# Trunk layer in fp32 on one core: where the row sums of the shared MLP pieces stand in the engines' order, and 64 weight columns in two HGRN2 products

## The chip, the cores and the metric

The kernel runs on one core of a Trainium2 chip. The metric is the device time of one execution in microseconds (us). The time before is the median of three runs. A profiled execution has its own time; its trace gives, for every engine, when each instruction began, how long it took and what ended the idle time before it. The engines are PE (TensorE matmuls, with PEld for its weight loads), DVE (VectorE), ACT (ScalarE), POOL (GpSimd) and SP (SyncE, which here only issues DMAs). ACT issues DMAs too.

## What is computed

One layer of a hybrid encoder over 1024 tokens of width 1024, with 16 meta tokens in front. One input projection feeds three mixers: HGRN2 (6 heads of 64), Mamba-2 (6 heads) and S5 (16 groups). Their outputs are concatenated, projected by w_out, added to the scaled input and normalised; a squared-ReLU MLP of width 4096 and a second normalisation follow.

```python
proj = h @ w_in[l]
q_a, f_a, i_a, g_a, z_b, xbc_b, dt_b, u_c = jnp.split(proj, split_idx, axis=-1)
...
mixed = jnp.concatenate([y_a, y_b, y_c], axis=-1).astype(h.dtype) @ w_out[l]
h = layer_norm(ALPHA * h + mixed, ln1_g[l], ln1_b[l])
ff = jnp.square(jax.nn.relu(h @ w_mlp_in[l])) @ w_mlp_out[l]
h = layer_norm(ALPHA * h + ff, ln2_g[l], ln2_b[l])
```

HGRN2 works in chunks; inside a chunk, token t reads token s with a decay that depends on both and on the key dimension:

```python
o_inter = jnp.einsum('bhtk,bhkv->bhtv', qc * jnp.exp(G), state)
diff = G[:, :, :, None, :] - G[:, :, None, :, :]
decay = jnp.exp(jnp.where(causal[:, :, None], diff, -jnp.inf))
scores = jnp.einsum('bhtsk,bhsk->bhts', qc[:, :, :, None, :] * decay, kc)
o_intra = jnp.einsum('bhts,bhsv->bhtv', scores, vc)
```

## The kernel before

**Products in three matmuls.** fp32 numbers are split into a high and a low half of a shorter type. `mm3` (L107 to L110) multiplies with three matmuls: high weight by high data (L108), high by low (L109), low by high (L110). A row of the trace names them as output<-moving operand, weights. Here `hi`, `lo`, `h1b`, `fh` and `fl` are such halves; `pm_o`, `pg`, `pm_sc` are PSUM tiles. `pm_o` and `pm_sc` have two buffers each and `pg` three.

**Weights.** `load_raw` (L182) has SP load a block of 128 by 512 (256 KB) into `raw`, a ring of four buffers. `split` has ACT cast the high half (L100), then DVE subtract to get the low half (L87). A raw buffer comes free when its low half is made.

**Order.** All engines work in order. The tile scheduler sets the order of instructions on each engine when the kernel is built; a row that waits holds everything behind it on its engine, and a DMA issue on SP that waits for a buffer holds the issues behind it.

**Stages.** Tokens are in two halves of 512. Until some 340 us the input projection, S5 and the first half of HGRN2 and Mamba-2 run together; until some 440 us w_out of half 0 and its layer norm; until some 650 us the second half of HGRN2 and Mamba-2 beside four MLP pieces of half 0 (512 hidden units each). Eight HGRN2 chunks of 128 tokens are handled in all. Then w_out of half 1 follows: `wout_units(1, ...)` gives eight sums, the four token tiles t4 to t7 for the first 512 columns (dh0), then the same for dh1; each is 24 matmuls and ends in an accumulate on DVE, `acc<-acc,pm_o` (L90). The layer norms and transposes (`norm1`, `h1_transpose`) of half 1 run beside the last eight sums of the pieces of half 0. Then piece 0 of half 1: its products with w_mi, and eight sums with w_mo of 12 matmuls each.

**Shared pieces.** From about 778 us pieces 4 to 7 are computed for both halves at once by a Strassen scheme (`up_strassen`). It needs differences and sums of blocks of the two halves' activations, the row sums, made by `row_sums` (L1246): `fetch3` loads two blocks of `b_d` (the stored activations) into `ar`, a pool of eight buffers; `third` subtracts one from the other on DVE, splits the result on ACT and DVE, and ACT stores both halves to `T_d` number 3. `first`, `second` and `fourth` make the others. `stream(n)` (L1239) has SP read `T_d` number n back into the `h1a` tiles, four loads of 512 KB. Weight differences are made beside: `w5` adds two raw w_mi blocks on DVE into `tw` (L84), which is then split.

**Where the row sums stand before.** `run(a, b)` interleaves two lists of units in the order of the code: the eight w_out sums and the eight units of `fetch3` and `third`. In piece 0 a string of letters sets the order by hand: u and w are its products, f and n the units of `first` and `second`, s is `stream(1)`, and d its eight sums.

**HGRN2's levels.** `hg_level` computes the scores of a chunk by levels of width 1 to 64. Levels below 64 use 64 weight columns on each half of the array, `ps[hms[x]]` (L791). The last level (L783) uses 64 weight columns and 128 moving ones, on one half only, and ACT copies the result to `Py` (L785). `hg_out` (L810) sums q times k per token by two moving columns, `ind2`, with 128 weight columns.

Of the kernel before, what the change touches and what calls it, by code (L numbers as in the profile page):

```python
# [66 lines left out]
def tile_trunk(ctx, tc, xT, x_tok, w_vdt, w_ch, w_out, w_mi, w_mo, glu_w, pack, kconst,  # L67
# [15 lines left out]
    def add(e, out, a, b):  # L83
        e.tensor_tensor(out=out, in0=a, in1=b, op=ALU.add)  # L84

# [3 lines left out]
    def stt(out, a, s, b, op0, op1):  # L89
        V.scalar_tensor_tensor(out=out, in0=a, scalar=s, in1=b, op0=op0, op1=op1)  # L90

# [90 lines left out]
    def load_raw(src):  # L182
        rings.append(rings.pop(0))
        raw = rings[-1]()
        nc.sync.dma_start(out=raw, in_=src)
        return raw

    def load_h(src, dst=None):
# [588 lines left out]
    def hg_level(c, h):  # L777
        hb = HB[c % len(HB)]
        ps = p_sc()
        if h == 64:  # L780

            for ct in range(3):
                PE.matmul(ps[0:64, ct * 128:ct * 128 + 128].rearrange("p (g l) -> p g l", g=2),  # L783
                          hb["B"][:, ct, 0:64], hb["A"][:, ct, :, 64:128], start=True, stop=True, skip_group_check=True)
            S.copy(hb["Py"][0:64], ps[0:64, 0:384].rearrange("p (h l) -> p h l", h=6))  # L785
        else:
# [18 lines left out]
    def hg_out(c):  # L805
# [3 lines left out]
        for ct in range(3):  # L809
            PE.matmul(po[:, 384 + 2 * ct:386 + 2 * ct], hb["QK"][:, ct], ind2, start=(ct == 0), stop=False,  # L810
                      skip_group_check=True)
        for h in range(6):
# [261 lines left out]
    def mix_in(half, k):  # L1074
        src_d, o = ((mixA_d, 0), (mixB_d, 3), (mixC_d, 6))[k // 3]
        raw = load_raw(src_d[:, k - o, HALF * half:HALF * half + HALF])
        split(hk(half, 0, POS[k]), hk(half, 1, POS[k]), raw)

    def accumulate(t, dh, lhs, w, first, c0=0, nc_=512):

        cs = slice(512 * dh + c0, 512 * dh + c0 + nc_)
        ps = p_o()[:, 0:nc_]
        n = len(w)
        for j in range(n):
            mm3(ps, lhs[j][0], lhs[j][1], w[j][0][:, c0:c0 + nc_], w[j][1][:, c0:c0 + nc_], j == 0, j == n - 1)
        if first:
            stt(acc[t][:, cs], acc[t][:, cs], ALPHA, ps, ALU.mult, ALU.add)
        else:
            add(V, acc[t][:, cs], acc[t][:, cs], ps)

# [155 lines left out]
    def row_sums(t2h, t2l, pool):  # L1246
# [38 lines left out]
        def units(f):  # L1285
            return [lambda k=k: f(k) for k in range(4)]

        return units(fetch3) + units(third), units(first) + [lambda: stream(1)] + units(second), units(fourth)

    def up_strassen(js, A, t2, again, ahead, beside):  # L1290

# [77 lines left out]
        def keep(f, half):  # L1369
            return lambda i, p: S.copy(tile_(f, half, i), p)  # L1370
# [7 lines left out]

        us += [w5] + go("c", "s1", "1", True, keep(1, 0)) + [lambda: stream(3)] + beside[:2]
        us += [w1] + go("a", "11", "11", True, keep(0, 1)) + beside[2:]  # L1380
# [8 lines left out]

    def strassen_units(fs, ts_, keep, b_op, sums=None, again=False, beside=()):  # L1390

# [162 lines left out]
        if sums is not None:  # L1554
            us += up_strassen(js, A, sums, again, ahead, list(beside))
        else:
# [110 lines left out]
    sums = row_sums(t2h, t2l, ff2)  # L1667
    run(wout_units(1, (6, 7, 0, 1, 2, 3, 4, 5), True), sums[0])
    run(sum([[lambda t=t: norm1(t), lambda t=t: h1_transpose(t)] for t in h1_], []), pre[cut:])
# [3 lines left out]
    p0 = piece(0, [1], (), HALF, True)  # L1673
    for c in "u u f u w f u f f d d s n d n d n d n d d d".split():
        (p0 if c in "udw" else sums[1]).pop(0)()
    for p in range(NPRE, NP):
        js = list(range(NF * p, NF * p + NF))
        for f in strassen_units((js[:2], js[2:]), (list(h0), list(h1_)), True, lambda name: [None] * 2, (t2h, t2l), p < NP - 1,
                                sums[2] if p == NPRE else ()):
            f()  # L1680
# [110 lines left out]
```

## Time and profile before

| | |
|---|---|
| three runs | 1223.6, 1224.56 and 1226.91 us |
| median | 1224.56 us |
| profiled execution, its own time | 1227.8 us |
| its span, first to last instruction | 1225.7 us |
| mean granted TensorE clock | 0.994 |
| HBM traffic | 148.43 MB read, 30.24 MB written |

A row of a timeline gives the start, the duration, engine and line, the operation, output<-input, the size and, in brackets, how long the engine was idle before it and what ended that. A matmul row lasts longer than the step to the next one, since matmuls overlap: the pace is read from starts. An fp32 matmul that is not split in halves stands as two instructions in the trace. An SP row's duration is the time from its first issue to its last.

### The profile page before, as it was taken

To read this page: it belongs to the slowest core of one execution; us is meant where nothing else is said; L and a number is where in the kernel's file an instruction comes from. 1 tells how busy PE (TensorE), PEld (TensorE's weight loads), DVE (VectorE), ACT (ScalarE), POOL (GpSimd) and SP (SyncE) were. 2 spreads that over 40 slices of the span, in tenths; PEclk is the share of its full clock that TensorE was granted. 3 is DMA by queue.
4 is the path that set the end of the run, shared out by engine and by line. 5 is a ranking of instruction groups with operands and counts; after the bars stand their busy time and mean duration, and the time that the engine had idled before them with its cause. 6 is when DMAs were issued, how large, how long until landed. Compare 5 with 4: busy or idle time off the path is not lost.

```text
span 1225.7 us, 19167 instructions
## 1 busy us (share of the span) xinstructions
PE 1194.5 (97%) x6932; PEld 984.8 (80%) x6932; DVE 898.6 (73%) x1953; ACT 596.0 (49%) x1312; POOL 24.5 (2%) x35
## 2 busy tenths in 40 slices
PE   8999999999999999999998998999999999999997
PEld 8988788778787888887886886878878778788886
DVE  7824866787777797757564776779597796899956
ACT  5343233544775376545453354463553635546542
POOL 0000000000000000000000000000000000003003
PEclk9999999999999999999998999999999999999999
DMA  8142343224557252323159367863635627357331
GB/s 272 55 148 86 78 122 114 104 85 131 164 187 233 65 151 81 100 79 113 52 170 324 100 180 235 266 198 103 237 106 188 224 71 252 124 160 243 121 112 68
DMA packets 111693, 180.97 MB, mean 148 GB/s; under 512 B 10992, under 2 KB 45424, under 8 KB 111600
## 3 DMA queue, kind: packets, MB, share of 16 engines
q1 hardware_dynamic: 108144, 173.47, 44.5%
q10 hardware_dynamic: 3456, 6.29, 1.3%
q8 instruction: 54, 0.88, 0.3%
q14 instruction: 39, 0.32, 0.1%
HBM read 148.43 MB, written 30.24 MB: 146 GB/s over the span
## 4 chain that ended last, share of the span: by engine, by line
PE 70%; DMA 13%; DVE 11%; ACT 3%; issue 2%; SPq 1%; ACTq 0%; POOL 0%; POOLq 0%; DVEq 0%
PE pg L108 11%; PE pg L109 11%; PE pg L110 11%; PE pm_o L108 7%; PE pm_o L109 7%; PE pm_o L110 7%; DMA raw<-w_mi 4%; PE pm_sc L109 2%; PE pm_sc L110 2%; PE pm_sc L108 2%; PE pm_sc L791 2%; DMA raw<-w_out 2%; DVE lo L87 1%; DMA xr<-xT 1%; DMA raw<-w_mo 1%
## 5 line engine op out<-in xcount | busy, mean ns | idle before, releaser
L87 DVE TENSOR_TENSOR lo<-raw,hi 128x512 fp32r<-128x512 f32 x260 | 177.1, 692 | 120.4 <-ACT hi L100 117.3
L100 ACT CAST hi<-raw 128x512 fp32r<-128x512 f32 x260 | 159.1, 619 | 181.7 <-PE pg L109 79.5
L108 PE MATMUL pm_o<-hi,fh 128*128 128x512 f32 x232 | 94.0, 405 | 3.6 <-DVE acc L90 3.3
L110 PE MATMUL pm_o<-hi,fl 128*128 128x512 f32 x232 | 91.6, 395 | 0.0
L109 PE MATMUL pm_o<-lo,fh 128*128 128x512 f32 x232 | 91.6, 395 | 0.0
L108 PE MATMUL pg<-x0h,hi 128*128 128x264 f32 (+1 forms) x264 | 85.3, 323 | 0.4 <-ACT uch L640 0.4
L108 PE MATMUL pg<-h1a,hi 128*128 128x512 f32 (+1 forms) x224 | 82.7, 370 | 2.2 <-ACT hi L100 1.4
L110 PE MATMUL pg<-x0h,lo 128*128 128x264 f32 (+1 forms) x264 | 84.5, 320 | 0.1
L109 PE MATMUL pg<-x0l,hi 128*128 128x264 f32 (+1 forms) x264 | 83.9, 318 | 0.0
L109 PE MATMUL pg<-h1a,hi 128*128 128x512 f32 (+1 forms) x224 | 81.2, 363 | 0.7 <-DMA h1a<-T_d 0.7
L110 PE MATMUL pg<-h1a,lo 128*128 128x512 f32 (+1 forms) x224 | 81.4, 364 | 0.0
L110 PE MATMUL pg<-h1b,lo 128*128 128x512 f32 x176 | 68.6, 390 | 0.1
L108 PE MATMUL pg<-h1b,hi 128*128 128x512 f32 x176 | 68.5, 389 | 0.0
L109 PE MATMUL pg<-h1b,hi 128*128 128x512 f32 x176 | 68.5, 389 | 0.0
L109 PE MATMUL pg<-x1l,hi 128*128 128x512 f32 x168 | 66.4, 395 | 0.0
L110 PE MATMUL pg<-x1h,lo 128*128 128x512 f32 x168 | 66.3, 395 | 0.0
L108 PE MATMUL pg<-x1h,hi 128*128 128x512 f32 x168 | 66.2, 394 | 0.0
L84 DVE TENSOR_TENSOR acc<-acc,pm_o 128x512 f32<-128x512 f32 (+1 forms) x77 | 52.0, 675 | 18.6 <-PE pm_o L110 17.6
L100 ACT CAST fh<-ar 128x512 fp32r<-128x512 f32 (+1 forms) x72 | 39.5, 560 | 40.5 <-DVE ar L87 32.0
L100 ACT CAST hi<-tw 128x512 fp32r<-128x512 f32 x52 | 31.9, 620 | 51.4 <-DVE tw L87 28.9
L108 PEld LDWEIGHTS pm_o<-hi,fh 128*128 128x128 f32 x232 | 44.1, 190 | 13.4 <-DVE acc L90 3.8
L108 PEld LDWEIGHTS pg<-x0h,hi 128*128 128x128 f32 x264 | 49.6, 188 | 5.2 <-ACT uch L640 0.8
(459 smaller groups left out, 3042.7 us busy)
## 6 DMA issues: line engine op xcount, KB each, us to landing
raw<-w_mo SPq DMA_DIRECT2D x140, 256.0 KB, 3.4
raw<-w_mi SPq DMA_DIRECT2D x112, 256.0 KB, 3.3
h1a<-T_d SPq DMA_DIRECT2D x48, 512.0 KB, 6.4
raw<-w_ch SPq DMA_DIRECT2D x48, 256.0 KB, 3.3
raw<-w_out SPq DMA_DIRECT2D x32, 256.0 KB, 3.8
acc<-x_tok SPq DMA_DIRECT2D x8, 512.0 KB, 5.5
b_d<-sig SPq DMA_DIRECT2D x16, 256.0 KB, 3.0
ar<-b_d SPq DMA_DIRECT2D x16, 256.0 KB, 5.3
```

What stands on the lines that cost most here:

```text
L84: e.tensor_tensor(out=out, in0=a, in1=b, op=ALU.add)
L87: e.tensor_tensor(out=out, in0=a, in1=b, op=ALU.subtract)
L100: S.copy(hi, src)
L108: PE.matmul(out, wh, xh, start=start, stop=False, **kw)
L109: PE.matmul(out, wh, xl, start=False, stop=False, **kw)
L110: PE.matmul(out, wl, xh, start=False, stop=stop, **kw)
L791: PE.matmul(ps[hms[x], ct * 64:ct * 64 + 64].rearrange("p (g b l) -> p g b l", g=2, l=h), hb["B"][:, ct, hms[x]], Av, start=True, stop=Tru ...
```

## The change

Four things are done. `load_raw` now keeps its last DMA in `fetched`, and `accumulate` keeps each accumulate's instruction in `sums_done`; `behind(f, n)` issues the units of `f` after the accumulate n places before the latest. `tc.issue_after` adds order on the same engine alone, no wait.

1. Five of the eight w_out sums are written first. The four `fetch3` units stand behind the last w_out load on SP. Each `third` stands behind the accumulate two before the latest that is written (`sums_done[-3]`).
2. `stream(1)` leaves piece 0's string and stands in the first shared piece behind `w5`; there, `w5` stands behind the fifth of the eight accumulates of piece 0 (`sums_done[-4]` when it is written).
3. HGRN2's last level uses, per pair of heads, two matmuls of 64 weight and 64 moving columns, one on each half of the array, and two copies to `Py` in place of one.
4. The q times k sums use 64 weight columns on each half, 6 matmuls in place of 3.

```diff
-        nc.sync.dma_start(out=raw, in_=src)
+        fetched[0] = nc.sync.dma_start(out=raw, in_=src)
         return raw
...
             for ct in range(3):
-                PE.matmul(ps[0:64, ct * 128:ct * 128 + 128].rearrange("p (g l) -> p g l", g=2),
-                          hb["B"][:, ct, 0:64], hb["A"][:, ct, :, 64:128], start=True, stop=True, skip_group_check=True)
-            S.copy(hb["Py"][0:64], ps[0:64, 0:384].rearrange("p (h l) -> p h l", h=6))
+                for g in range(2):
+                    PE.matmul(ps[hms[g], ct * 64:ct * 64 + 64], hb["B"][:, ct, 0:64], hb["A"][:, ct, g, 64:128],
+                              start=True, stop=True, skip_group_check=True)
+            Pg = hb["Py"].rearrange("p (c g) l -> p c g l", g=2)
+            for g in range(2):
+                S.copy(Pg[0:64, :, g], ps[hms[g], 0:192].rearrange("p (c l) -> p c l", c=3))
...
-            PE.matmul(po[:, 384 + 2 * ct:386 + 2 * ct], hb["QK"][:, ct], ind2, start=(ct == 0), stop=False,
-                      skip_group_check=True)
+            for x in hms:
+                PE.matmul(po[x, 384 + 2 * ct:386 + 2 * ct], hb["QK"][:, ct, x], ind2, start=(ct == 0), stop=False,
+                          skip_group_check=True)
...
+    sums_done = []
+
+    def behind(f, n):
+
+        with tc.issue_after(sums_done[-1 - n].ins):
+            f()
...
         if first:
-            stt(acc[t][:, cs], acc[t][:, cs], ALPHA, ps, ALU.mult, ALU.add)
+            sums_done.append(stt(acc[t][:, cs], acc[t][:, cs], ALPHA, ps, ALU.mult, ALU.add))
         else:
-            add(V, acc[t][:, cs], acc[t][:, cs], ps)
+            sums_done.append(add(V, acc[t][:, cs], acc[t][:, cs], ps))
...
-        us += [w5] + go("c", "s1", "1", True, keep(1, 0)) + [lambda: stream(3)] + beside[:2]
+        if first:
+            us += [lambda: behind(w5, 3), lambda: stream(1)]
+        else:
+            us.append(w5)
+        us += go("c", "s1", "1", True, keep(1, 0)) + [lambda: stream(3)] + beside[:2]
...
-    run(wout_units(1, (6, 7, 0, 1, 2, 3, 4, 5), True), sums[0])
+
+    wu = wout_units(1, (6, 7, 0, 1, 2, 3, 4, 5), True)
+    for f in wu[:5]:
+        f()
+    for f in sums[0][:4]:
+        with tc.issue_after(fetched[0].ins):
+            f()
+    for i in range(4):
+        if wu[5 + i:]:
+            wu[5 + i]()
+        behind(sums[0][4 + i], 2)
...
-    for c in "u u f u w f u f f d d s n d n d n d n d d d".split():
+    for c in "u u f u w f u f f d d n d n d n d n d d d".split():
...
-        for f in strassen_units((js[:2], js[2:]), (list(h0), list(h1_)), True, lambda name: [None] * 2, (t2h, t2l), p < NP - 1,
+        for f in strassen_units((js[:2], js[2:]), (list(h0), list(h1_)), True, lambda name: [None] * 2, (t2h, t2l), p == NPRE, p < NP - 1,
```

What this does to the order of instructions is shown at three places. The first is DVE in w_out of half 1. The numbers tell buffers apart; `acc4` to `acc7` are the token tiles t4 to t7, `raw_7355` is the eighth w_out block of dh0 before, `ar` the blocks of `b_d`. Before:

```order
L87 TENSOR_TENSOR lo_7348<-raw_7345,hi_7347 128x512
L87 TENSOR_TENSOR h1b12_7266<-raw_7351,h1b02_7263 128x512
L87 TENSOR_TENSOR ar_7452<-ar_7450,ar_7452 128x512
L87 TENSOR_TENSOR lo_7358<-raw_7355,hi_7357 128x512
L87 TENSOR_TENSOR fl_7627<-ar_7452,fh_7626 128x512
L87 TENSOR_TENSOR fl_7222<-sig_7248,fh_7221 128x512
L87 TENSOR_TENSOR ar_7483<-ar_7481,ar_7483 128x512
L90 SCALAR_TENSOR_TENSOR acc4_7267<-acc4_7267,pm_o_7362 128x512
```

A subtraction of `third` stands ahead of the low half of the eighth block, another one ahead of the first accumulate. After, the same stretch (`raw_7411` is the eighth block):

```order
L87 TENSOR_TENSOR fl_7234<-sig_7260,fh_7233 128x512
L87 TENSOR_TENSOR lo_7404<-raw_7401,hi_7403 128x512
L87 TENSOR_TENSOR h1b12_7322<-raw_7407,h1b02_7319 128x512
L87 TENSOR_TENSOR lo_7414<-raw_7411,hi_7413 128x512
L87 TENSOR_TENSOR fl_7278<-sig_7304,fh_7277 128x512
L90 SCALAR_TENSOR_TENSOR acc4_7323<-acc4_7323,pm_o_7418 128x512
L1125 BN_STATS bst_7721<-acc4_7323 128x6
L90 SCALAR_TENSOR_TENSOR acc5_7324<-acc5_7324,pm_o_7445 128x512
```

No row of `ar` is left in it. The first two subtractions of `third` after, around the first accumulate of dh1:

```order
L90 SCALAR_TENSOR_TENSOR acc7_7326<-acc7_7326,pm_o_7499 128x512
L87 TENSOR_TENSOR lo_7558<-raw_7555,hi_7557 128x512
L87 TENSOR_TENSOR lo_7564<-raw_7561,hi_7563 128x512
L87 TENSOR_TENSOR lo_7570<-raw_7567,hi_7569 128x512
L87 TENSOR_TENSOR ar_7601<-ar_7599,ar_7601 128x512
L87 TENSOR_TENSOR fl_7643<-ar_7601,fh_7642 128x512
L90 SCALAR_TENSOR_TENSOR acc4_7323<-acc4_7323,pm_o_7573 128x512
L87 TENSOR_TENSOR ar_7605<-ar_7603,ar_7605 128x512
```

They stand behind the last accumulate of dh0 and the low halves of all dh1 blocks.

The second place is DVE in the eight sums of piece 0. The rows whose output is `tw` from two `raw` tiles are the additions of `w5`; `raw_8315` to `raw_8327` are w_mo blocks. Before:

```order
L90 SCALAR_TENSOR_TENSOR acc4_7267<-acc4_7267,pm_o_8230 128x512
L84 TENSOR_TENSOR tw_8394<-raw_8395,raw_8397 128x512
L90 SCALAR_TENSOR_TENSOR acc5_7268<-acc5_7268,pm_o_8244 128x512
L87 TENSOR_TENSOR lo_8401<-tw_8394,hi_8400 128x512
L90 SCALAR_TENSOR_TENSOR acc6_7269<-acc6_7269,pm_o_8271 128x512
L84 TENSOR_TENSOR tw_8404<-raw_8405,raw_8407 128x512
L87 TENSOR_TENSOR lo_8324<-raw_8321,hi_8323 128x512
L87 TENSOR_TENSOR lo_8330<-raw_8327,hi_8329 128x512
L87 TENSOR_TENSOR lo_8411<-tw_8404,hi_8410 128x512
L90 SCALAR_TENSOR_TENSOR acc7_7270<-acc7_7270,pm_o_8290 128x512
```

The first addition stands behind the first accumulate. After:

```order
L90 SCALAR_TENSOR_TENSOR acc6_7325<-acc6_7325,pm_o_8319 128x512
L87 TENSOR_TENSOR lo_8372<-raw_8369,hi_8371 128x512
L87 TENSOR_TENSOR lo_8378<-raw_8375,hi_8377 128x512
L90 SCALAR_TENSOR_TENSOR acc7_7326<-acc7_7326,pm_o_8338 128x512
L90 SCALAR_TENSOR_TENSOR acc4_7323<-acc4_7323,pm_o_8381 128x512
L84 TENSOR_TENSOR tw_8442<-raw_8443,raw_8445 128x512
L84 TENSOR_TENSOR tw_8452<-raw_8453,raw_8455 128x512
L87 TENSOR_TENSOR lo_8449<-tw_8442,hi_8448 128x512
L87 TENSOR_TENSOR lo_8459<-tw_8452,hi_8458 128x512
L90 SCALAR_TENSOR_TENSOR acc5_7324<-acc5_7324,pm_o_8400 128x512
```

Both stand behind the fifth, one behind the other.

The third place is SP in the first shared piece, at the loads of `T_d` number 4. Before:

```order
L185 DMA raw_8727<-w_mo 128x512
L185 DMA raw_8729<-w_mo 128x512
L185 DMA raw_8736<-w_mi 128x512
L185 DMA raw_8742<-w_mi 128x512
L185 DMA raw_8858<-w_mo 128x512
L185 DMA raw_8864<-w_mo 128x512
L1244 DMA h1a00_8612<-T_d4_2244 128x1024
L1244 DMA h1a10_8614<-T_d4_2244 128x1024
L1244 DMA h1a01_8613<-T_d4_2244 128x1024
L1244 DMA h1a11_8615<-T_d4_2244 128x1024
```

Two w_mi loads and two w_mo loads stand ahead of them. After:

```order
L185 DMA raw_8783<-w_mo 128x512
L185 DMA raw_8785<-w_mo 128x512
L1257 DMA h1a10_8670<-T_d4_2244 128x1024
L1257 DMA h1a00_8668<-T_d4_2244 128x1024
L1257 DMA h1a01_8669<-T_d4_2244 128x1024
L1257 DMA h1a11_8671<-T_d4_2244 128x1024
L185 DMA raw_8792<-w_mi 128x512
L185 DMA raw_8798<-w_mi 128x512
L185 DMA raw_8914<-w_mo 128x512
L185 DMA raw_8920<-w_mo 128x512
```

Those four loads now stand behind. PE's order is the same but for the doubled rows of HGRN2, and small shifts beside them.

More of the change, by code (lines that the diff above doesn't have):

```diff
@@ L83, in add @@
     def add(e, out, a, b):
-        e.tensor_tensor(out=out, in0=a, in1=b, op=ALU.add)
+        return e.tensor_tensor(out=out, in0=a, in1=b, op=ALU.add)
     def sub(e, out, a, b):
@@ L89, in stt @@
     def stt(out, a, s, b, op0, op1):
-        V.scalar_tensor_tensor(out=out, in0=a, scalar=s, in1=b, op0=op0, op1=op1)
+        return V.scalar_tensor_tensor(out=out, in0=a, scalar=s, in1=b, op0=op0, op1=op1)
     def ts(e, out, a, s1, s2=None, op0=ALU.mult, op1=None):
@@ L184, in load_raw @@
         raw = rings[-1]()
-        nc.sync.dma_start(out=raw, in_=src)
+        fetched[0] = nc.sync.dma_start(out=raw, in_=src)
         return raw
+    fetched = [None]
     def load_h(src, dst=None):
@@ L1286, in units, with up_strassen @@
             return [lambda k=k: f(k) for k in range(4)]
-        return units(fetch3) + units(third), units(first) + [lambda: stream(1)] + units(second), units(fourth)
-    def up_strassen(js, A, t2, again, ahead, beside):
+        return units(fetch3) + units(third), units(first) + units(second), units(fourth)
+    def up_strassen(js, A, t2, first, again, ahead, beside):
         us = []
@@ L1388, in up_strassen, with strassen_units @@
         return us
-    def strassen_units(fs, ts_, keep, b_op, sums=None, again=False, beside=()):
+    def strassen_units(fs, ts_, keep, b_op, sums=None, first=False, again=False, beside=()):
         us = []
@@ L1554, in strassen_units @@
         if sums is not None:
-            us += up_strassen(js, A, sums, again, ahead, list(beside))
+            us += up_strassen(js, A, sums, first, again, ahead, list(beside))
         else:
```

## The prediction

> **What bounds the kernel now.** The page's table of engines comes first: PE is busy for nearly all of the span, so time is won only where PE stands still, runs at a lower granted clock, or has less to do.
>
> ```profile
> PE 1194.5 (97%) x6932; PEld 984.8 (80%) x6932; DVE 898.6 (73%) x1953; ACT 596.0 (49%) x1312; POOL 24.5 (2%) x35
> ```
>
> The busy time by 100 us windows (columns: PE, PEld, DVE, ACT, POOL, each with its count, then granted clock, DMA share, GB/s) says where. The stretch in which HGRN2 chunks and MLP pieces of half 0 share the engines has no hole at all; the next one, with w_out of half 1, has 4 us of holes and a dip of the clock.
>
> ```profile
> 500.00:600.00 100.00, 100.00 (x707) 80.10 (x705) 63.42 (x151) 55.02 (x148) 0.00 (x0) 1.00 0.29 88
> 600.00:700.00 100.00, 95.85 (x500) 78.36 (x500) 59.95 (x115) 39.00 (x85) 0.00 (x0) 0.97 0.53 175
> ```
>
> The yardstick for a hole is the undisturbed pace of the 512-wide matmuls. From the first matmul of one Strassen product to the first of the next, 24 matmuls, the timeline of PE shows 5.44 us, that is 0.227 us each:
>
> ```profile
> 778.09 0.39 PE L108 MATMUL pm_sc<-h1a,hi 128*128 128x512 f32 x1
> ...
> 783.53 0.39 PE L108 MATMUL pg<-h1b,hi 128*128 128x512 f32 x1
> ```
>
> **Stall 1, in w_out of half 1.** PE's timeline:
>
> ```profile
> 656.77 0.50 PE L108 MATMUL pm_o<-hi,h1b 128*128 128x512 f32 x1
> 661.42 0.80 PE L109 MATMUL pm_o<-lo,h1b 128*128 128x512 f32 x1 [4.15 <-DVE lo L87]
> ...
> 667.56 0.42 PE L108 MATMUL pm_o<-hi,h1b 128*128 128x512 f32 x1
> ```
>
> At pace, L109 would have begun at 657.00; it began 4.42 later. Then the 14 matmuls from 661.42 to 667.56 took 6.14 instead of 3.18, another 2.96: the clock had been lowered behind the hole (window of 4 us below). Together 7.4 us. Who was late stands in the timelines of DVE, ACT and SP:
>
> ```profile
> 660.07 0.69 DVE L87 TENSOR_TENSOR ar<-ar 128x512 f32<-128x512 f32 x1 [4.61 <-DMA ar<-b_d]
> 660.68 0.68 DVE L87 TENSOR_TENSOR lo<-raw,hi 128x512 fp32r<-128x512 f32 x1
> ```
> ```profile
> 656.10 0.62 ACT L100 CAST hi<-raw 128x512 fp32r<-128x512 f32 x1 [1.11 <-DMA raw<-w_out]
> ```
> ```profile
> 651.11 0.33 SPq L185 DMA_DIRECT2D raw<-w_out  x1
> ...
> 656.09 0.84 SPq L1257 DMA_DIRECT2D ar<-b_d  x2
> ```
>
> The low half of the eighth w_out block needed only its high half, done at 656.72, but the subtraction of the fourth `third` sum stood ahead of it on DVE, and its two loads were issued only at 656.09.
>
> **The change, part by part.**
>
> *Row sums behind w_out.* `third` keeps its 8 loads, 4 subtractions and 4 splits; they move. On DVE none now stands ahead of a low half of the first eight blocks; on SP none stands ahead of any of the 16 w_out loads. With the block's landing unchanged (656.1), cast 0.62 and subtraction 0.68 end at about 657.45 with their hand-overs, 0.45 after need. I expect the load itself to come earlier, since the fetches that shared SP's queue and the DMA with it are gone, and take 0.2 of stall left: −7.2, bounds −6.9 and −7.4. If a hole of 0.45 stays, the clock should not dip for it: the hole at 812 (below) is longer and its window reads 1.00. Past the queue of SP: the next eight fetches, which refill the same 8 buffers, now stand ahead of the second four w_mo blocks and wait for the moved subtractions.
>
> ```profile
> 682.06 21.23 SPq L185 DMA_DIRECT2D raw<-w_mo  x8
> 703.80 4.49 SPq L185 DMA_DIRECT2D raw<-w_mi  x3
> ```
>
> Those eight w_mo issues took 21 us, since their ring came free so slowly; eight fetches that pass before the fifth of them cost nothing, if the subtractions are done by about 693.
>
> *The step ahead of piece 0's sums.* PE and DVE:
>
> ```profile
> 759.04 0.39 PE L110 MATMUL pm_o<-hi,fl 128*128 128x512 f32 x1
> 762.76 0.50 PE L108 MATMUL pm_o<-hi,fh 128*128 128x512 f32 x1 [3.33 <-DVE acc L90]
> ...
> 766.44 0.46 PE L108 MATMUL pm_o<-hi,fh 128*128 128x512 f32 x1
> ```
> ```profile
> 761.42 0.69 DVE L84 TENSOR_TENSOR tw<-raw 128x512 f32<-128x512 f32 x1 [5.18 <-DMA raw<-w_mi]
> ...
> 765.74 0.69 DVE L84 TENSOR_TENSOR tw<-raw 128x512 f32<-128x512 f32 x1 [1.66 <-DMA raw<-w_mi]
> ```
>
> L108 was due at 759.27: 3.49 lost. The 9 matmuls up to 766.44 took 3.68 for 2.04: 1.64 more. Together 5.1. The accumulate of a finished sum stood behind the weight addition of `w5`, which waited for its load. Now both additions stand behind the fifth accumulate: no accumulate is left behind a load here. What is late next: without the 5.1 the product behind the sums starts at 773.0 on this scale instead of 778.1, and the fifth sum, three sums of 2.72 earlier, ends at 764.8; the second pair lands at 765.7, so the additions end by 767.1, cast and low half by about 769. The product that reads them has 4 us to spare, so I take the full −5.1; the other bound is 0, the same lateness met there.
>
> *The T4 load.* The reads of T_d3 and T_d4 now each stand ahead of w_mi loads that stood ahead of them:
>
> ```profile
> 811.86 0.39 PE L110 MATMUL pg<-h1a,lo 128*128 128x512 f32 x1
> ...
> 814.08 0.50 PE L109 MATMUL pg<-h1a,hi 128*128 128x512 f32 x1 [0.67 <-DMA h1a<-T_d]
> ```
> ```profile
> 797.31 0.86 SPq L185 DMA_DIRECT2D raw<-w_mi  x2
> 801.18 0.80 SPq L185 DMA_DIRECT2D raw<-w_mo  x2
> 802.03 2.15 SPq L1244 DMA_DIRECT2D h1a<-T_d  x4
> ```
>
> Two steps took 2.22 instead of 0.45: 1.8 lost, because the four issues waited behind w_mi and w_mo loads that waited for their ring. Ahead of those they could go by 797.3, 4.7 us earlier, if their tiles are free; the weights behind them then start up to 2.15 later, the length of the four issues. Bounds −1.8 and +2.15; the weights were ahead of need here, so −1.4.
>
> *HGRN2's last level.* 3 fp32 matmuls of 64 weight and 128 moving columns become 6 of 64 by 64, the form of the lower levels. PE's rows (an fp32 matmul is two instructions in the trace):
>
> ```profile
> 253.40 0.87 PE L783 MATMUL pm_sc<-A,B 128*64 128x128 f32 x6
> 254.20 0.50 PE L109 MATMUL pg<-x1l,hi 128*128 128x512 f32 x1
> ```
> ```profile
> 237.23 0.57 PE L791 MATMUL pm_sc<-A,B 128*64 128x64 f32 x12
> 237.73 0.50 PE L110 MATMUL pg<-x0h,lo 128*128 128x512 f32 x1
> ```
> ```profile
> 272.75 0.92 PE L791 MATMUL pm_sc<-A,B 128*64 128x64 f32 x24
> 273.60 0.39 PE L108 MATMUL pg<-x0h,hi 128*128 128x264 f32 x1
> ```
>
> The block holds PE for 0.80; a block of 12 in the new form for 0.50, and 12 more add 0.35. 8 chunks × 0.30 = −2.4; it is real time, since these stretches have no holes. The other bound is 0, if the form gained nothing here.
>
> *The q·k sums.* 6 instructions of 128 weight columns become 12 of 64, with 2 moving columns:
>
> ```profile
> 287.02 0.72 PE L810 MATMUL pm_o<-kc,QK 128*128 128x2 f32 x6
> 287.67 0.27 PE L814 MATMUL pm_o<-v,P 128*64 128x64 f32 x1
> ```
>
> From L810 to the next block 0.65. Behind a 128-column stream the new block should cost no more than L791's 0.50, and the 64-column work behind it joins on as the second dozen above did: −0.15 × 8 = −1.2. Bounds: −0.30 each (0.35 for the dozen), −2.4; above, each instruction pair at twice what it costs now, +0.65 each, +5.2. I take the value near L791, whose weights have the same 64 columns. The Trainium skill, TensorEngine Tiling (Array Packing), section Instruction Overhead, speaks against this edit: a fixed cost of about 60 cycles per matmul, and "Don't take tiling factor from a dimension that's already small". By it the sum would lose this −1.2 and more; the second dozen of L791 at 0.35, which is 0.029 each, speaks for a small fixed cost.
>
> *The copy of that level.* One copy becomes two of half the size:
>
> ```profile
> L785 ACT COPY Py<-pm_sc x8: 472/473/477, 254.3 to 609.5; 64x384 f32<-64x384 f32 x8
> ```
>
> The scores are whole later by between 0 and one more such copy, 0.47. ACT has room, but in the first chunk the matmul that reads them now stands right behind two stream matmuls: +0.3 in sum, at most 8 × 0.47 = +3.8, at least 0.
>
> *DVE after the move.* Of `third`, 8 operations of 0.68, 5.4 us, land in the stretch from the first dh1 sum to the transposes:
>
> ```profile
> 704.00:712.00 8.00, 8.00 (x41) 6.69 (x40) 7.96 (x16) 4.52 (x10) 0.00 (x0) 1.00 0.68 197
> ```
>
> DVE is full there, yet PE does not wait: the layer norms run far ahead of their transposes. I book +0.8 of new stall; bounds 0 and 5.4.
>
> **The sum.** −7.2 −5.1 −1.4 −2.4 −1.2 +0.3 +0.8 = −16.2. The profiled execution took 1227.8 (span 1225.7 and 2.1 around it), so 1211.6; it lies 3.2 above the median of the three runs, 1224.56, and I put the same distance on the forecast: 1208.4.
>
> **The clock in the sum.** 4.6 us of it (2.96 and 1.64) are not holes but slow matmuls behind holes. The windows show the clock at 0.60 behind the 4.15 us hole and at 1.00 around the short ones of T4:
>
> ```profile
> 660.00:664.00 4.00, 2.58 (x6) 2.12 (x7) 3.81 (x6) 1.73 (x3) 0.00 (x0) 0.60 0.95 315
> ...
> 812.00:816.00 4.00, 2.67 (x11) 1.80 (x10) 1.10 (x2) 2.41 (x5) 0.00 (x0) 1.00 0.19 74
> ```
>
> So the other runs of before may have paid less behind the 3.33 us hole, by up to 1.6. The Trainium skill, TensorE: Matmul & The Clock Gate, section "What's actually happening", says that the gate falls after a free-running idle window of about 3.4 us; by it the 3.33 us hole would often cost only itself, and the sum would be −14.6. Here the clock fell behind it too.
>
> **Rivals.**
>
> *One of the two big holes comes back elsewhere* (0.22). For it: DMA is busy for 0.95 of the window at 660, so loads that no longer wait in the queue may wait in flight; DVE is full at 704; w5's low halves have only 4 us. Against: each replay above leaves a margin. Then 5 to 7 of the sum are lost, −10 is left: 1214.6.
>
> *HGRN2's edits cost as the fixed price per matmul has it* (0.10). With +0.65 × 8 for q·k and nothing from the level the sum is −16.2 + 3.6 + 5.2 = −7.4: 1217.
>
> *No gain* (0.05). The w_out loads are bound by bandwidth, not by their place: the row sums' 2 MB (8 loads of 256 KB) only change places with later weights, and the holes go with them. HGRN2's −3.6 meets the copies at their upper bound, +3.8. 1225.
>
> *Slower: DVE held by the moved row sums* (0.05). Their loads now queue behind all 16 w_out loads, the last four of which were issued when their buffers came free:
>
> ```profile
> 678.05 2.37 SPq L185 DMA_DIRECT2D raw<-w_out  x4
> ```
> ```profile
> ar<-b_d SPq DMA_DIRECT2D x16, 256.0 KB, 5.3
> ```
>
> So they land near 686, and on DVE the first stands ahead of the first dh1 accumulate:
>
> ```profile
> 686.87 0.69 DVE L90 SCALAR_TENSOR_TENSOR acc<-acc,pm_o 128x512 f32<-128x512 f32 x1 [1.79 <-PE pm_o L110]
> ```
>
> The two PSUM buffers of the sums cover one sum, 5.4 us, more. From 692 on each us of hold is a us of PE, and holes as long as the two big ones bring slow matmuls of about 3. Four pairs that each land a whole 5.3 after the one before would hold DVE for 21.2: 21.2 − 5.4 + 2 × 3 − 16.2 = +5.6, 1230. Against it: the eight are issued together, so that only the first is waited for.
>
> **How the numbers follow.** The forecast has 0.58, its own range 1204 to 1212. The range runs from 1203 (every term at its better end, −19.1, is 1205.5, and the three runs spread by up to 2.4 around their median) to 1220, which takes in the first two rivals; it leaves out the last two and half of the tail. A measurement of this kernel can tell about 0.3%, 3.7 us, from no change. Faster by more: 0.58 + 0.22 + 0.10 − 0.02 = 0.88. Within: 0.07. Slower: 0.05.
>
> **What would show it.** Right: no PE row with idle over 1 us between 650 and 790 on the changed kernel, granted clock 1.00 there, L786 blocks at 0.50, L816 blocks not above 0.65. Wrong: a PE row released by DVE acc or lo between 680 and 730 (the moved sums), by DVE lo at the first shared product (w5), by ACT Py (the two copies), or L816 blocks near 1.2.

## The result, and the profile after

The changed kernel takes 1215.47 us (median of four runs, 1212.58 to 1216.77), the kernel before in the same comparison 1225.72 (1223.6 to 1226.91). The ratio is 0.9911, 95% interval 0.9890 to 0.9931: 10.3 us faster. Measured once more beside other kernels it was again 1215.47, ratio 0.9906 (0.9883 to 0.9928). The forecast was 1208.4, its range 1203 to 1220.

The profiled execution after took 1212.6 (span 1210.7), the lowest of its four runs; that of before took 1227.8, more than all four of its own. So the two traces differ by 15.2 us, and the medians by 10.3. Terms below come from the traces, and are then held against kernels with one part of the change each.

The clock in 40 slices dipped before:

```profile
PEclk9999999999999999999998999999999999999999
```

The page after, its engines and the clock, which no longer dips:

```profile
PE 1184.9 (98%) x7028; PEld 976.2 (81%) x7028; DVE 897.3 (74%) x1953; ACT 596.7 (49%) x1320; POOL 24.9 (2%) x35
...
PEclk9999999999999999999999999999999999999999
```

The two big holes are gone. These are PE's rows of after at the places where the low half of the eighth w_out block and the third sum of piece 0 had been waited for; no idle time stands behind them, and the steps are 0.23:

```profile
650.65 0.39 PE L108 MATMUL pm_o<-hi,h1b 128*128 128x512 f32 x1
650.87 0.39 PE L109 MATMUL pm_o<-lo,h1b 128*128 128x512 f32 x1
...
748.81 0.39 PE L110 MATMUL pm_o<-hi,fl 128*128 128x512 f32 x1
749.04 0.39 PE L108 MATMUL pm_o<-hi,fh 128*128 128x512 f32 x1
```

HGRN2's blocks after, the last level first, then q·k (each with the row behind it):

```profile
252.68 0.57 PE L786 MATMUL pm_sc<-A,B 128*64 128x64 f32 x12
253.18 0.50 PE L109 MATMUL pg<-x1l,hi 128*128 128x512 f32 x1
...
285.58 0.52 PE L816 MATMUL pm_o<-kc,QK 128*64 128x2 f32 x12
285.95 0.25 PE L820 MATMUL pm_o<-v,P 128*64 128x64 f32 x1
```

A level holds PE for 0.50 in place of 0.80, and so in seven of the eight chunks; the eighth goes from 0.66 to 0.35. The q·k block shown holds it for 0.37 in place of 0.65. But the stream matmul just ahead of the block tells against part of that. Before, then after:

```profile
286.79 0.39 PE L110 MATMUL pg<-x1h,lo 128*128 128x512 f32 x1
```
```profile
285.26 0.39 PE L110 MATMUL pg<-x1h,lo 128*128 128x512 f32 x1
```

Before, the block began 0.23 behind that matmul (at 287.02), after 0.32 behind it (at 285.58). So this block gains 0.28 − 0.09 = 0.19. Four of the eight stand in such a place. Of the others one gains some 0.5, two 0.1 or less, and one, which has a wait right behind it, nothing: some 1.5 us for all eight.

New waits have come. Two stand in the w_mo sums beside the layer norms, one in the first shared piece:

```profile
695.10 0.50 PE L108 MATMUL pm_o<-hi,fh 128*128 128x512 f32 x1 [0.81 <-DVE acc L90]
...
699.03 0.50 PE L108 MATMUL pm_o<-hi,fh 128*128 128x512 f32 x1 [0.87 <-DVE acc L84]
...
780.65 0.50 PE L108 MATMUL pg<-h1a,hi 128*128 128x512 f32 x1 [1.53 <-ACT ar L1383]
```

The table follows the same matmul through both traces. The lead is the start before minus the start after.

| the matmul followed | before | after | lead | step |
|---|---|---|---|---|
| ahead of the first block of HGRN2 that was changed | 235.77 | 235.35 | 0.4 | |
| ahead of the first hole | 656.77 | 650.65 | 6.1 | +5.7 |
| behind it and its slow matmuls | 670.35 | 656.77 | 13.6 | +7.5 |
| behind the w_mo sums beside the layer norms | 717.47 | 707.63 | 9.8 | −3.8 |
| ahead of the second hole | 759.04 | 748.81 | 10.2 | +0.4 |
| behind it and its slow matmuls | 767.43 | 751.99 | 15.45 | +5.2 |
| behind the wait at 780 of after | 795.77 | 782.15 | 13.6 | −1.8 |
| behind the wait at 797 of after (0.33) | 811.86 | 799.13 | 12.7 | −0.9 |
| where before waited for T4 (`T_d` number 4) | 814.41 | 799.82 | 14.6 | +1.9 |
| behind the wait at 812 of after (0.52) | 827.13 | 813.80 | 13.3 | −1.3 |
| the last such matmul | 1217.24 | 1202.23 | 15.0 | +1.7 |

The wait at 695 ends with an accumulate that stood on DVE behind layer norm work; from 689.87 to it DVE has no idle time:

```profile
689.87 1.92 DVE L87 TENSOR_TENSOR lo<-raw,hi 128x512 fp32r<-128x512 f32 x3 [0.79 <-ACT hi L100]
...
693.16 1.28 DVE L90 SCALAR_TENSOR_TENSOR acc<-acc,lrs,gb 128x1024 f32<-128x1024 f32 x1
694.36 0.68 DVE L90 SCALAR_TENSOR_TENSOR acc<-acc,pm_o 128x512 f32<-128x512 f32 x1
```

Where the wait at 699 comes from is seen on SP, ACT and DVE of after:

```profile
681.34 5.50 SPq L1270 DMA_DIRECT2D ar<-b_d  x8
690.59 2.29 SPq L185 DMA_DIRECT2D raw<-w_mo  x4
```
```profile
695.77 1.96 ACT L100 CAST hi<-raw 128x512 fp32r<-128x512 f32 x3 [4.09 <-DMA raw<-w_mo]
```
```profile
696.42 0.69 DVE L87 TENSOR_TENSOR lo<-raw,hi 128x512 fp32r<-128x512 f32 x1 [1.26 <-ACT hi L100]
...
698.29 0.68 DVE L84 TENSOR_TENSOR acc<-acc,pm_o 128x512 f32<-128x512 f32 x1
```

The fifth w_mo block, issued at 690.59, was there at 695.77, 5.2 us later, and so too late to have made the wait at 695. DVE waited for it with its low half, and the accumulate that PE needed at 699 stood behind. Before, that block took from 699.81 to 702.42, 2.6 us:

```profile
699.81 3.48 SPq L185 DMA_DIRECT2D raw<-w_mo  x4
```
```profile
702.42 0.62 ACT L100 CAST hi<-raw 128x512 fp32r<-128x512 f32 x1 [1.19 <-DMA raw<-w_mo]
```

The 4 us windows (last columns: granted clock, DMA share, GB/s) show the DMA at this place; since PE is some 13 us ahead in after, the window of before that belongs to 688 is the one at 700. From 688 to 700, where most of the layer norms ran, before had a DMA share of 0.04 and less; after, from 676 to 688, has 0.86 to 1.00, with what was moved. Before, then after:

```profile
700.00:704.00 4.00, 4.00 (x19) 3.30 (x19) 3.99 (x8) 2.10 (x6) 0.00 (x0) 1.00 0.63 198
704.00:708.00 4.00, 4.00 (x24) 3.39 (x23) 4.00 (x9) 2.84 (x6) 0.00 (x0) 1.00 0.62 197
```
```profile
688.00:692.00 4.00, 3.47 (x14) 2.32 (x14) 3.21 (x7) 2.46 (x6) 0.00 (x0) 1.00 0.96 357
692.00:696.00 4.00, 3.19 (x19) 2.50 (x18) 3.16 (x7) 0.23 (x1) 0.00 (x0) 1.00 0.91 306
```

And the wait at 780, on SP and ACT of after: the 2 MB of T3 (`T_d` number 3) stand between two pairs of w_mi loads, the second pair takes until 779.5, its cast holds ACT, and the copy that frees a PSUM buffer stands behind the cast.

```profile
765.54 1.54 SPq L185 DMA_DIRECT2D raw<-w_mi  x2
767.13 4.16 SPq L1257 DMA_DIRECT2D h1a<-T_d  x4
771.90 2.20 SPq L185 DMA_DIRECT2D raw<-w_mi  x2
```
```profile
779.50 0.62 ACT L100 CAST hi<-raw 128x512 fp32r<-128x512 f32 x1 [5.19 <-DMA raw<-w_mi]
780.02 0.58 ACT L1383 COPY ar<-pg 128x512 f32<-128x512 f32 x1
```

### The profile page after: what moved, and what is told of

It reads as the page before. It is cut to its first block, busy times and chain, and to the rows that moved or that the text cites. A ratio compares the mean times of both kernels' runs of the same rounds, so it can differ in the third digit from the quotient of the medians.

```text
span 1210.7 us, 19370 instructions
## 1 busy us (share of the span) xinstructions
PE 1184.9 (98%) x7028; PEld 976.2 (81%) x7028; DVE 897.3 (74%) x1953; ACT 596.7 (49%) x1320; POOL 24.9 (2%) x35
## 4 chain that ended last, share of the span: by engine, by line
PE 74%; DMA 10%; DVE 9%; ACT 4%; issue 2%; SPq 0%; ACTq 0%; POOL 0%; POOLq 0%; DVEq 0%
PE pg L108 13%; PE pg L109 13%; PE pg L110 13%; PE pm_o L108 6%; PE pm_o L110 5%; PE pm_o L109 5%; DMA raw<-w_mi 5%; PE pm_sc L109 2%; PE pm_sc L110 2%; PE pm_sc L108 2%; PE pm_sc L796 2%; DVE lo L87 2%; ACT hi L100 1%; PE pv L108 1%; PE pv L110 1%
## 5 line engine op out<-in xcount | busy, mean ns | idle before, releaser
L108 PEld LDWEIGHTS pm_o<-hi,fh 128*128 128x128 f32 x232 | 43.6, 188 | 12.7 <-DVE acc L84 1.6
```

Of the source, the lines that this page charges most:

```text
L108: PE.matmul(out, wh, xh, start=start, stop=False, **kw)
```

## The experiments

**One part of the change at a time.** First the row sums of w_out alone.

It is the kernel before with this part of the change's diff:

```diff
-    run(wout_units(1, (6, 7, 0, 1, 2, 3, 4, 5), True), sums[0])
+    wu = wout_units(1, (6, 7, 0, 1, 2, 3, 4, 5), True)
...
+    for f in sums[0][:4]:
+        with tc.issue_after(fetched[0].ins):
+            f()
...
+        behind(sums[0][4 + i], 2)
```

> The kernel before with the row sums alone moved (fetches behind the last w_out load, third behind the accumulates). Theory, by the offsets of the two profiles: the hole in w_out of half 1 goes (7.4 us), 3.4 us come back as waits of PE for DVE in the eight w_mo sums that run beside the layer norms, the hole in piece 0's sums stays (about 5 us). About 4 us faster than before, 0.997. Rival, the moved work is free and the 3.4 us came from the other parts: 7 us faster, no wait over 0.3 us in those sums. Rival, the late load itself decides: no gain, the hole of w_out reappears a block later.

Measured: 1223.4 us against 1225.9, 2.5 us by the medians; the ratio, 0.9970 (0.9954 to 0.9986), makes it 3.7 us. No hole is left in w_out; the waits in the w_mo sums are there (0.79 and 0.66). What was not expected is that the second hole grew from 3.33 to 4.47:

```profile
760.67 0.80 PE L108 MATMUL pm_o<-hi,fh 128*128 128x512 f32 x1 [4.47 <-DVE acc L90]
```

PE came to that sum 3.1 us earlier than in before; the load that DVE waits for came 2.1 us earlier (its addition at 759.33, 761.42 before), and the difference is given back there.

Then the step of the first shared piece alone, likewise on the kernel before.

```diff
-    "u u f u w f u f f d d s n d n d n d n d d d"
+    "u u f u w f u f f d d n d n d n d n d d d"
-        us += [w5] + go("c", "s1", "1", True, keep(1, 0)) + [lambda: stream(3)] + beside[:2]
+        if first:
+            us += [lambda: behind(w5, 3), lambda: stream(1)]
+        else:
+            us.append(w5)
+        us += go("c", "s1", "1", True, keep(1, 0)) + [lambda: stream(3)] + beside[:2]
```

> The kernel before with the step of the first shared piece alone moved (w5 behind the fifth accumulate, stream(1) behind it). Theory: the hole in piece 0's sums goes (5.2 us), the T4 wait goes (1.4 us), and two new waits of PE for ACT in the first shared piece cost 1.4 and 0.6 us, since T3's load now stands ahead of the w_mi loads on SP. The hole in w_out stays. About 4.5 us faster, 0.996. Rival, the new ACT wait belongs to the earlier arrival of PE (row sums): then it is absent here and the gain is 6.5 us.

Measured: 1224.05, 1.9 us by the medians; ratio 0.9977 (0.9961 to 0.9993), 2.8 us. The second hole is gone, and the waits in the shared piece are longer than in the changed kernel:

```profile
790.72 0.50 PE L108 MATMUL pg<-h1a,hi 128*128 128x512 f32 x1 [2.28 <-ACT ar L1379]
...
808.61 0.50 PE L108 MATMUL pg<-h1a,hi 128*128 128x512 f32 x1 [1.28 <-ACT hi L100]
```

So they belong to this part, not to PE's earlier arrival.

HGRN2's two edits alone (`hg_level` and `hg_out` as in the diff of the change).

> The kernel before with the two HGRN2 edits alone. Theory: a level block falls from 0.80 to 0.50 and a q times k block from 0.65 to 0.37 on PE, eight of each: 2.4 + 2.2 = 4.6 us, with up to 1.3 us more from the blocks beside them; both big holes stay. 4.6 to 6 us faster, 0.9955. Rival by a fixed price per matmul: no gain or slower.

Measured: 1220.92, ratio 0.9959 (0.9942 to 0.9976), 5.0 us by both. The rival, no gain or slower by a fixed price per matmul, is refuted. By the ratios the three parts make 3.7 + 2.8 + 5.0 = 11.5 us together; all at once made 10.9 and, in the repeat, 11.5. By the medians it is 2.5 + 1.9 + 5.0 = 9.4 against 10.3 and 10.4. Within the intervals, some 2 us for each part, they add.

**The changed kernel again**, unchanged.

> The changed kernel as it is, once more, for a second profile and more runs. Its profiled run (1212.6) was the fastest of its four (to 1216.8), while the profiled run of before was the slowest of its three. Theory: the median gain is about 10 to 12 us, and runs above 1215 have a hole of 3 us or more with a dip of the clock behind it, in the w_mo sums or in the first shared piece. Rival: all runs lie near 1212.6 and the slower ones were chance.

Measured: 1215.47 (1214.25 to 1217.91), 0.9906. Its profiled execution, 1214.25, is again the lowest, and has the same waits in other sizes (0.81 and 0.34 in the w_mo sums, 1.28 and 1.14 in the shared piece) and no hole over 1.3 us between 650 and 1000. The mean granted clock over its six runs goes from 0.998 to 0.995, and the run with 0.995 is the slowest. So the slower runs may have more slow matmuls, but no trace shows where.

**What makes the waits in the w_mo sums?** The first theory was DVE's new work. Third's operations on POOL:

```diff
-            sub(V, b[k][1], b[k][0], b[k][1])
+            sub(G, b[k][1], b[k][0], b[k][1])
-            split(*o, x)
+            split(*o, x, G if n == 3 else V)
```

> The changed kernel with third's 8 operations (subtraction and low half) on POOL, which is idle there, in place of DVE. Theory (DVE is full from 688 to 715, so the moved operations cost PE the 3.4 us in the w_mo sums): the two waits of PE for DVE acc near 695 and 699 go, 2 to 3 us faster than the changed kernel, ratio to before about 0.988. Rival 1 (these waits come from PE's earlier arrival at the layer norms, not from the moved operations): no change, 0.991. Rival 2 (POOL and DVE slow each other): the DVE operations beside them get longer, slower than the changed kernel.

Measured: 1218.79, ratio 0.9930 (0.9913 to 0.9947), 2 to 3 us slower than the changed kernel. POOL takes 1.29 for what DVE does in 0.68, ACT's casts wait for it, and a small ACT step of the layer norm stands behind the casts; DVE waits for that step with the accumulates behind it (DVE, then PE):

```profile
686.89 0.22 DVE L90 SCALAR_TENSOR_TENSOR rs_t<-rs_y,rs_h 128x1 f32<-128x1 f32 x1 [5.42 <-ACT rs_y L169]
```
```profile
694.44 0.47 PE L108 MATMUL pm_o<-hi,fh 128*128 128x512 f32 x1 [2.81 <-DVE acc L90]
```

So this run doesn't answer the question. The next kernel leaves the operations out, so that the third row sum is not computed:

```diff
-            sub(V, b[k][1], b[k][0], b[k][1])
-            away(3, k, b[k][1])
+            o = pool.tile([128, 512], F32R, tag="fh", name="fh")
+            S.copy(o, b[k][1])
+            for j in range(2):
+                S.dma_start(out=T_d[3][:, j, k], in_=o.bitcast(F32))
```

> The changed kernel with third's 8 DVE operations left out (ACT casts the fetched block, and the cast is stored twice; so the third row sum and what follows from it are not computed). Theory: as for POOL, without its side effects: both DVE waits go, 3.0 to 3.4 us faster than the changed kernel, 0.988. Rival: no change, 0.991.

Measured: 1216.22, ratio 0.9911 (0.9892 to 0.9930): no gain. The waits are still there, 0.39 and 1.04:

```profile
695.84 0.50 PE L108 MATMUL pm_o<-hi,fh 128*128 128x512 f32 x1 [0.39 <-DVE acc L90]
...
699.91 0.50 PE L108 MATMUL pm_o<-hi,fh 128*128 128x512 f32 x1 [1.04 <-DVE acc L84]
```

DVE's new work alone does not make them. The DMA windows above gave the next theory: the eight fetches for `first` and `second`, 2 MB, that stand ahead of the last four w_mo loads. In the next kernel they stand behind them.

```diff
     run(sum([[lambda t=t: norm1(t), lambda t=t: h1_transpose(t)] for t in h1_], []), pre[cut:])
+    gate.append(fetched[0])
...
-            nc.sync.dma_start(out=b, in_=b_d[half][:, k])
+            if gate:
+                with tc.issue_after(gate[0].ins):
+                    nc.sync.dma_start(out=b, in_=b_d[half][:, k])
+            else:
+                nc.sync.dma_start(out=b, in_=b_d[half][:, k])
```

> The changed kernel with the second eight fetches of b_d put behind all eight w_mo loads on SP. Leaving third's DVE work out did not remove the waits, so the theory now is: the DMA decides. From 672 to 696 it is 0.91 to 1.00 busy in the changed kernel (0.00 to 0.04 from 688 to 700 before), the fifth w_mo load takes 5.2 us in place of 2.6, and DVE stands at its low half with the accumulates behind it. Then the wait near 699 (DVE acc L84) goes and most of that near 695 stays or shrinks: 1 to 2 us faster than the changed kernel, ratio to before 0.989 to 0.990. Rival (DVE's own queue of layer norms, whatever the loads): waits unchanged, 0.991. Rival (the fetches are now late for the first row sum): a new wait in piece 0, slower than 0.991.

Measured: 1215.62, ratio 0.9915 (0.9893 to 0.9938): no gain in time. Both waits are gone in its trace, one of 0.77 came at the next sum (703), and through the w_mo sums PE loses 2.1 us where it lost 3.8 in the changed kernel. That gain of 1.7 is given back at the wait of the shared piece, which grows from 1.53 to 2.55 and now brings slow matmuls behind it:

```profile
781.86 0.79 PE L108 MATMUL pg<-h1a,hi 128*128 128x512 f32 x1 [2.55 <-ACT ar L1389]
782.45 0.63 PE L109 MATMUL pg<-h1a,hi 128*128 128x512 f32 x1
782.88 0.63 PE L110 MATMUL pg<-h1a,lo 128*128 128x512 f32 x1
```
```profile
776.00:780.00 4.00, 3.31 (x15) 2.42 (x13) 0.00 (x0) 0.00 (x0) 0.00 (x0) 1.00 1.03 408
780.00:784.00 4.00, 2.14 (x5) 1.75 (x6) 2.61 (x5) 3.29 (x7) 0.00 (x0) 0.73 0.32 121
```

The same without third's DVE operations (its sum is not computed):

> The same with third's 8 DVE operations left out as well (its sum is not computed). If loads and DVE work each hold one of the two waits, both go: 2.5 to 3.4 us faster than the changed kernel, 0.9885. If the loads alone decide: the same as with the late fetches alone. If neither: 0.991.

Measured: 1215.81, ratio 0.9921 (0.9898 to 0.9943). The waits in the w_mo sums are 0.41 and 0.25, and PE loses 2.5 us through them; that of the shared piece is 2.90.

**What makes the wait in the shared piece?** T3's loads behind the w_mi loads of the step after:

```diff
+        def late3():
+            with tc.issue_after(fetched[0].ins):
+                stream(3)
-        us += go("c", "s1", "1", True, keep(1, 0)) + [lambda: stream(3)] + beside[:2]
+        us += go("c", "s1", "1", True, keep(1, 0)) + ([] if first else [lambda: stream(3)]) + beside[:2]
...
-        us += [w7] + go("a", "s3", "3", False, total(1, 0)) + [lambda: stream(4)]
-        us += [w2] + go("b", "12", "21", True, total(0, 1))
+        us += [w7] + ([w2, late3] if first else []) + go("a", "s3", "3", False, total(1, 0)) + [lambda: stream(4)]
+        us += ([] if first else [w2]) + go("b", "12", "21", True, total(0, 1))
```

> The changed kernel with the loads of T3 put behind the two w_mi loads of the next step on SP (that step is written ahead of the product that reads T3), as they stood before. Theory (the two new waits in the first shared piece come from w_mi loads that are late because T3's and T4's 2 MB stand ahead of them, which hold ACT's casts and with them its PSUM copies): the wait of PE for the ACT copy near 780 goes, and the one near 797 may; 1.4 to 2 us faster than the changed kernel, 0.989 to 0.9895. Rival (T3 itself is then late): a wait of PE for h1a<-T_d in the first shared piece, no gain or slower.

Measured: 1215.89, ratio 0.9909 (0.9891 to 0.9926): no gain. The wait at 780 is gone, and two others have its place, one for the same kind of copy and one for T3 itself:

```profile
777.26 0.50 PE L108 MATMUL pg<-t2h,hi 128*128 128x512 f32 x1 [1.12 <-ACT ar L1383]
...
783.07 0.50 PE L109 MATMUL pg<-h1a,hi 128*128 128x512 f32 x1 [0.81 <-DMA h1a<-T_d]
```

Third on POOL and T3 late together:

> Both together, third on POOL and T3 behind the w_mi loads: if both theories hold and the terms add, 4 to 5 us faster than the changed kernel, 0.9865 to 0.987. If PE's earlier arrival turns the gain into waits on loads, less than that: 0.989.

Measured: 1218.69, ratio 0.9929 (0.9908 to 0.9950); POOL's cost decides, as in the kernel with POOL alone.

Late fetches and late T3 together:

> The changed kernel with both: the second eight fetches behind the w_mo loads, and T3's loads behind the next two w_mi loads. Theory now: what PE saves ahead of the first shared piece is given back there, since that piece waits on a chain of loads (w_mi, T3's 2 MB, again w_mi) that runs at a DMA share of about 1. With the late fetches alone the hole near 780 grew from 1.53 to 2.55 us, with a dip of the clock. Without that hole (T3 late) the 2 us saved in the w_mo sums should stay: 1 to 2.5 us faster than the changed kernel, ratio to before 0.989. Rival (the bytes decide, not their order): other holes in the piece take it, 0.991.

Measured: 1214.86, ratio 0.9913 (0.9887 to 0.9939), the lowest median of all, and not to be told from the changed kernel. Waits of 1.20, 0.82, 0.88 and 0.50 stand between 775 and 809. That agrees with the rival, by which the bytes of that stretch decide and not their order; no run takes bytes away, so it isn't shown.

Last, late fetches with w5 behind the second accumulate (`behind(w5, 6)`).

> The late fetches, with w5 behind the second of the eight accumulates in place of the fifth, which also puts T3's and T4's loads behind the w_mi loads again. Theory: w5's additions, and with them the whole chain of weights of the shared piece, come some 3 us earlier, the third accumulate may wait up to 1 us for the first addition's load; the hole near 780 goes, T4's wait of 1 to 2 us may return. 1 to 3 us faster than the changed kernel, 0.9885 to 0.990. Rival: the addition's load is as late as before (761 on before's scale), PE is 8 us earlier there, and the hole in piece 0's sums comes back with its clock dip: 3 to 5 us slower than the changed kernel, 0.995.

Measured: 1217.84, ratio 0.9930 (0.9908 to 0.9953), 2 to 3 us slower than the changed kernel. The rival held: the hole in piece 0's sums comes back, DVE first, then PE:

```profile
753.49 0.69 DVE L84 TENSOR_TENSOR tw<-raw 128x512 f32<-128x512 f32 x1 [5.38 <-DMA raw<-w_mi]
```
```profile
756.21 0.79 PE L108 MATMUL pm_o<-hi,fh 128*128 128x512 f32 x1 [3.36 <-DVE acc L90]
```

So standing behind the fifth accumulate is what that edit is worth: with the second, PE loses 6.5 us at this place on the changed kernel, and 1.8 come back at the wait of the shared piece.

This trace also bears on the question before, since its fetches are late too. Its fifth w_mo block was issued at 691.75 and there at 694.42, 2.7 us later. Even so PE waits in the w_mo sums, at the place of the first wait and at the sum that waited with the late fetches alone:

```profile
694.42 0.62 ACT L100 CAST hi<-raw 128x512 fp32r<-128x512 f32 x1 [2.73 <-DMA raw<-w_mo]
```
```profile
696.24 0.50 PE L108 MATMUL pm_o<-hi,fh 128*128 128x512 f32 x1 [0.81 <-DVE acc L90]
...
703.97 0.50 PE L108 MATMUL pm_o<-hi,fh 128*128 128x512 f32 x1 [0.77 <-DVE acc L84]
```

So the late fetches make the block land in 2.6 to 2.7 us, in all three kernels that have them and compute every sum, and in these three the second of the two waits is gone. The first does not hang on them: it is 0.81, 0.81 and 0.79 in the changed kernel, its repeat and the row sums alone, but 0.12 with T3 late alone, and none or 0.81 with late fetches. Through the w_mo sums PE loses 2.4 to 3.8 us where the fetches stand ahead, the kernels with operations on POOL apart, and 1.4 to 3.4 where they stand behind. What sets the first wait stays open.

## Why the prediction was right or wrong

*The two holes.* −7.2 and −5.1 forecast, −7.5 and −5.2 between the traces. The mechanism, in-order DVE held by a load with a ready operation behind it, is shown by each part alone and by the last kernel, which brings the second hole back. One reading of the first hole was wrong: the subtraction at 660.07 is the third of the four `third` sums, not the fourth. Its two loads are the pair issued at 652.08 and 653.51, the second of which landed at 659.98, not the pair of 656.09. So they were late by some 6.5 us in flight, at a DMA share of 0.90 and 1.03 in the 4 us windows from 652, more than by a late issue. Their place on DVE is what held the low half either way.

*HGRN2.* −2.4 −1.2 +0.3 forecast, −5.7 between the traces from the first changed block to w_out, and −5.0 by the medians. The level came out as worked out, −2.4. So, nearly, did q·k: some −1.5 where −1.2 was booked. The block itself gained 0.28, near the better bound of 0.30, but the stream matmul ahead of it pays 0.09 where it stood behind a stream; that price was not in the sum. Before, an instruction of 128 weight columns held PE for 0.108 (0.65 for 6), now one of 64 columns holds it for 0.031 (0.37 for 12). Whether the narrower weights or the two halves side by side did it was not tried apart. The rule of the Trainium skill, TensorEngine Tiling (Array Packing), section Instruction Overhead, was taken as a warning against this split; in this trace twice as many matmuls took less time. The rest, some 1 to 2 us, lies in the blocks beside and isn't settled. The copies of the level cost nothing that PE shows.

*DVE after the move.* +0.8 forecast, bounds 0 and 5.4; +3.8 between the traces, and 2.4 to 3.1 in three other traces that have this stage as it is. The size was inside the bounds, the term was booked too low. One step that failed is "eight fetches that pass before the fifth of them cost nothing". They cost no place in the queue; they cost the DMA, which the move had loaded to 0.91 and more just where the w_mo blocks arrive, and the fifth block took 5.2 us for 2.6. That is the wait at 699. The wait at 695 stood before that block had landed; it is about half with the 8 operations left out and comes and goes with the fetches late, so DVE's own queue seems to have a share in it, and what sets it stays open.

*The T4 load.* −1.4 forecast, bounds −1.8 and +2.15. The wait for T4 went whole (−1.9), but three waits in the same piece came (+1.8, +0.9, +1.3): +2.1 in sum, at the worse bound. "The weights were ahead of need here" was read from PE alone; ACT stands at those weights' casts with PSUM copies behind them, so a late weight is felt before its product needs it.

*From the profile to the median.* With minus for faster, the steps of the table give −0.4 −5.7 −7.5 +3.8 −0.4 −5.2 +2.1 −1.7 = −15.0, where −16.2 was forecast: 1212.6 against 1211.6 for the profiled executions. That the two come so close is partly luck. The 0.4 at the start and the 1.7 at the end lie where nothing was edited; in the trace of the repeat they are 0.9 and 0.4. The two terms that were booked too low, by 3.0 and 3.5, met gains in HGRN2 and at both ends that were not booked. The larger part of the miss is the step "I put the same distance on the forecast". The profiled execution of before lay above its median, that of after 2.9 below its own. The prices of the holes came from one execution; in others the second hole was 3.95 (HGRN2 alone) and 4.47 (row sums alone), and the first 3.27 to 4.15.

*The rivals.* What happened is nearest to the first, which gave 1214.6: what went came back in part elsewhere, not as one hole but as five small waits. Two of the prediction's own signs of being wrong are there: idle time of 1.53 at 780, where no row was to have over 1 us, and rows released by DVE's accumulates at 695 and 699. The slower mechanism, DVE held by late row sums, did not occur: DVE waited 0.79 us for the first pair. The granted clock is 1.00 in the windows of after shown here, as forecast.

## What to carry to other kernels

Moving loads out of the way of one stage puts their bytes into another: look at the DMA share of the stage they are moved to, not only at the queue they leave. When a hole is removed, the next load-bound stage takes part of the gain, since PE comes earlier and the load does not; here the late fetches saved 1.7 us in the w_mo sums and ended at the changed kernel's median. A block with a new shape is to be priced with the matmul ahead of it: q·k gained 0.28 inside and paid 0.09 there. One trace in which a wait is gone does not show its cause: a second kernel with late fetches had the first wait back. And a median is not to be forecast from one profiled execution by a fixed distance, when the terms are holes that differ by 1 us from run to run.

## What the runs showed of the hardware that was not expected

Slow matmuls came behind shorter holes than the 3.33 us of before, and not behind every hole of one length: none behind 2.01 (third without DVE) and 2.28 us (shared-piece step alone), some behind 1.68 (late fetches, third without DVE, at 1032), 2.16 (row sums alone, at 385), 2.33 (POOL), 2.55 (late fetches) and 2.90 us (late fetches, third without DVE), where steps of 0.43 us in place of 0.23 followed for up to 3.4 us. The shortest:

```profile
1032.32 0.50 PE L108 MATMUL pg<-h1a,hi 128*128 128x512 f32 x1 [1.68 <-ACT hi L100]
...
1033.50 0.63 PE L108 MATMUL pg<-h1a,hi 128*128 128x512 f32 x1
1033.93 0.63 PE L109 MATMUL pg<-h1a,hi 128*128 128x512 f32 x1
```

The granted clock of before is 0.50 in two stretches:

```profile
660.78:667.60 6.82, 6.18 (x15) 4.88 (x16) 4.40 (x7) 1.75 (x3) 0.00 (x0) 0.50 0.96 319
763.18:766.59 3.41, 3.41 (x10) 2.64 (x9) 1.75 (x4) 1.36 (x3) 0.00 (x0) 0.50 0.44 150
```

They last 2 × 3.41 and 3.41 us, and the 95.58 between them is 28 × 3.413; the other traces have no slow stretch of another length ahead of the last 20 us. So the clock changes on a fixed grid, and where a hole falls on it seems to count beside its length. The Trainium skill, TensorE: Matmul & The Clock Gate, section "What's actually happening", gives a free-running window of about 3.4 us; that spacing agrees with a free-running window, the holes of 1.68 to 2.90 us are shorter than the page leads one to expect.
